# Attention's sums of values taken for two blocks of queries at a time, and the weights of values 192 bytes further in their tiles

## The chip, the core and the metric

One core of a Trainium2 chip runs the whole program in one launch. The metric is the time of one execution on the device in microseconds (us); 2318.97 is the median of three runs of the kernel before. TensorE (PE in the profile) multiplies matrices: it loads a stationary operand (PEld rows) and streams a moving operand past it into PSUM. VectorE (DVE), ScalarE (ACT) and GpSimd (POOL) do the elementwise work, and SyncE (SP) issues the transfers.

## The reference

Two token sequences of 1024 x 1024 (a "prompt" and a "sample") go through two layers with shared weights. The first layer is a mix of retention heads and a state-space branch; the change meets it only in the tiles of its weights. The second is a neighbourhood attention of 16 heads of 64 over a 16 x 64 grid of tokens:

```python
def _odd_mixer(h, w_in, w_out, rel_bias):
    q, k, v, g = jnp.split(h @ w_in, 4, axis=-1)
    o = _neighbourhood_attention(q.reshape(hs), k.reshape(hs), v.reshape(hs), rel_bias)
    return (o * jax.nn.silu(g)) @ w_out
...
        s = jnp.einsum('bqhd,brkhd->bhqrk', qr, kb).astype(jnp.float32) * scale
        s = s + jnp.transpose(bias, (0, 2, 1, 3))[None]
        s = jnp.where(col_valid[:, None, :], s, NEG_INF)
        p = jax.nn.softmax(s.reshape(B, H, GRID_W, kr * GRID_W), axis=-1)
        return jnp.einsum('bhqrk,brkhd->bqhd', p, vb)
```

Before each layer the input is normalized, scaled and shifted; after it the result is normalized, gated and added to the input.

## The kernel before

**Precision.** A product of an activation h and a weight w is made of three matmuls in the type fp32r: w's rounded part times h's rounded part, and each one's rounded part times the other's rest (`dense`, `values`). So every block of 512 KB of weights is loaded into a tile `wr`, copied by ScalarE into `wh` (rounded) and subtracted by VectorE or GpSimd into `wl` (the rest), in `split`. `wr` has two buffers, `wh` and `wl` three each, all of 4096 bytes a partition. `dense` has the weights as the stationary operand and 512 columns of h moving: 24 matmuls for one half (512 tokens) of one block of 128 output columns. `values` makes v with its tokens on the partitions, so there h is the stationary operand and 256 columns of `wh` or `wl` move.

**Attention's steps.** `layer1` projects q, k, v and the gate for eight pairs of heads in each of two sequences (s = 0, 1), and after every half of a block of `dense` (and every quarter of `values`) it calls `unit`, which takes one step of the generator `na_mix`. A step deals with three blocks of 128 queries of one pair of heads at once. There are 8 blocks in a pair and 16 pairs, so 128 blocks, and the step i takes in this order

- the sums of values of block i-2: the transposed probabilities `pt0` and `pt1` move past 64 columns of `vn` (one for each head of the pair, each into its own half of the partitions of the PSUM bank `psc`, so the array is used as 128 x 64). That is 4 matmuls where the block is the first or last of its pair (2 tiles of keys) and 6 elsewhere (3 tiles of keys); the profile shows twice as many, since a matmul in plain fp32 is run in two passes;
- after four blocks, the product of `psc` with the gate `g2` on VectorE (L1253) and its store into `oD`;
- the transposes of block i-1 (`na_turn`, L136 into `psb`, copied to `pt0` by ScalarE and to `pt1` by VectorE);
- the scores of block i (`na_scores`: `psa`, L1199 adds the bias and finds the least, ACT's L1201 takes the exponential, L1202 and L1203 normalize on VectorE).

Then the next 24 (or 48) matmuls of the projection follow, and then the next step.

**What sets the order.** In `layer1` every matmul is held in the order of the program (`pin`), so TensorE's order is that of the code. The other engines' order is found by the framework's scheduler, which simulates the program. Between the two sequences, `load_h` brings the second sequence's h in over the first's; its copies run on ScalarE, VectorE and GpSimd. At the end the steps that are left are woven into `out_proj` of the first sequence, 12 matmuls between steps. Here both spans have names: the **seam** (the change of sequences) and the **weave**.

**Memory.** `MAP_L1` says in which 4096-byte slots (A0 to A21) and 8192-byte slots (E0 to E3) of SBUF the attention's tiles stand: `pt0` and `pt1` have two buffers each, in E3. Pools are laid out one behind another, the pool `w` (`wr`, `wh`, `wl`) ahead of all slots.

Of the kernel before, what the change touches and what calls it, by code (L numbers as in the profile page):

```python
# [13 lines left out]
F32R = mybir.dt.float32r  # L14
# [5 lines left out]
P = 128  # L20
# [18 lines left out]
def _parts(text):  # L39
# [39 lines left out]

MAP_L1 = _parts(  # L80
# [3 lines left out]
MAP_L1.update(  # L84
    kh0=_fulls("A11 A13"), kh1=_fulls("A16 A17"), q0=_fulls("A8 A3"), q1=_fulls("A4 A5"),
# [32 lines left out]
class Trunk:  # L118
# [89 lines left out]
        e = self.nc.gpsimd if eng == "P" else self.nc.vector  # L208
        e.tensor_tensor(lo, raw, hi.bitcast(F32), SUB)  # L209

    def w_block(self, src, shape, eng):
        raw = self.ring(self.wpool, shape, "wr")
        hi = self.ring(self.wpool, shape, "wh", F32R, 3)
        lo = self.ring(self.wpool, shape, "wl", F32R, 3)
        self.load(raw, src)
        self.split(hi, lo, raw, eng)
        return hi, lo
# [43 lines left out]

    def queue_values(self, w, c0):
        self.todo += [partial(self.w_block, w[512 * j:512 * j + 512, c0:c0 + 2 * P].rearrange("(k p) c -> p k c", p=P),
                              [P, 4, 256], "P") for j in range(2)]

    def values(self, vn, scale, done=None):

# [760 lines left out]
    def out_weights(self, w, ph, blks):  # L1028
        for k in range(8):
            tag = f"ow{k}"  # L1030
            raw = self.t([P, 1024], "st", F32, ph) if "st" in ph.map and k > 3 else self.ring(self.wpool, [P, 1024], "wr")
            if tag not in ph.map:
                hi, lo = (self.ring(self.wpool, [P, 1024], x, F32R, 3) for x in ("wh", "wl"))
            elif len(ph.map[tag]) == 1:
                hl = self.t([P, 2, 1024], tag, F32R, ph)
                hi, lo = hl[:, 0], hl[:, 1]
            else:
                hi, lo = (self.t([P, 1024], tag, F32R, ph) for _ in range(2))
            self.load(raw, w[k * P:(k + 1) * P, :])
            self.split(hi, lo, raw, "V" if k in (1, 3, 5, 6) else "P")  # L1040
            blks.append((hi, lo))
            yield
# [180 lines left out]
    def na_mix(self):  # L1223

        sbs, pts = {}, {}
        raw = first = mid = last = po = None
        n = 8 * 16
        for i in range(-2, n + 2):
            k, j = divmod(i + 2, 8)
            if k < 16:  # L1230
                if j == 0:
                    if not k:
                        raw = self.na_raw(0)
                    first = self.na_bias(raw, "bl", self.mask[1], P, EDGE)
                elif j == 1:
                    mid = self.na_bias(raw, "bm", self.mask[0], 0, WIDE)
                elif j == 2:
                    last = self.na_bias(raw, "br", self.mask[1], 0, EDGE)
                elif j == 3 and k < 15:
                    raw = self.na_raw((k + 1) % 8)  # L1240
            if 0 <= i - 2 < n:
                k, j = divmod(i - 2, 8)
                if j % 4 == 0:
                    po = self.pst("c")
                pt, b0 = pts.pop(i - 2), max(j - 1, 0)
                nk = 3 if 0 < j < 7 else 2
                for z in range(nk):
                    for a in range(2):
                        self.mm(po[64 * a:64 * a + 64, (j % 4) * P:(j % 4 + 1) * P], self.na[k]["vn"][:, b0 + z, 64 * a:64 * a + 64],
                                pt[a][:, z * P:(z + 1) * P], start=(z == 0), stop=(z == nk - 1))  # L1250
                if j % 4 == 3:
                    o, sl = self.t([P, 512], "o"), slice((j - 3) * P, (j + 1) * P)
                    self.nc.vector.tensor_tensor(o, po, self.na[k]["g2"][:, sl], MUL)  # L1253
                    s, p = divmod(k, 8)
                    self.store(self.oD[1, s][p * P:(p + 1) * P, sl], o)
            if 0 <= i - 1 < n:
                pts[i - 1] = self.na_turn(sbs.pop(i - 1), (i - 1) % 8)
            if 0 <= i < n:
                k, j = divmod(i, 8)
                sbs[i] = self.na_scores(self.na[k], first if j == 0 else last if j == 7 else mid, j)  # L1260
            yield
# [239 lines left out]
```

## Time and profile before

| what | value |
|---|---|
| median of 3 runs (lowest to highest) | 2318.97 us (2318.91 to 2320.42) |
| the profiled execution's own time | 2319.64 us |
| its span, first to last instruction | 2317.8 us |
| mean granted clock of TensorE | 0.984 |
| busy: PE, PEld, DVE, ACT, POOL | 96%, 80%, 59%, 37%, 34% |
| chain that ended last, by engine | PE 72%, DVE 11%, DMA 8%, POOL 3% |

The profiled execution is 0.67 us above the median. Layer 0 takes the first half of the span; attention's steps run from about 1187 us to about 2163 us of it, and the last `out_proj` ends the program. A busy PE is only a sign that something is in its pipeline: matmuls overlap, so what one costs is read from the starts of neighbours, not from its duration.

### The profile page before, as it was taken

The numbers are of one execution on the slowest core, as the hardware profiler recorded it, in microseconds if no ns is written. First come the engines' busy times: TensorE is split into PE (matmuls) and PEld (weight loads), VectorE is DVE, ScalarE is ACT, GpSimd is POOL, SyncE is SP. The second block draws the span as 40 slices with busy tenths as digits, with TensorE's granted clock in tenths as the row PEclk, the third lists the DMA queues.
The fourth block names the chain that finished last, engine by engine and source line by source line (L and its number), as shares of the span: only waits on it lengthen the run. The fifth ranks groups of instructions, "written<-read, shape, count | busy, mean of one in ns | idle before, by whom it ended". The sixth has DMA issues, their size and how long they took to land.

```text
span 2317.8 us, 35213 instructions
## 1 busy us (share of the span) xinstructions
PE 2216.5 (96%) x13248; PEld 1844.3 (80%) x13248; DVE 1374.4 (59%) x3013; ACT 853.7 (37%) x1842; POOL 785.1 (34%) x670
## 2 busy tenths in 40 slices
PE   6989988998999999999999999998999999998997
PEld 4757877786878888888988888887888888886786
DVE  4836888888899566575345545455545545457322
ACT  4532321223322244343344434355444444444211
POOL 2335555657665121456511111113111101113233
PEclk9999999999999999999999999999999999999999
DMA  9774232224221245435511111224111111114354
GB/s 316 248 229 135 74 88 45 67 81 139 56 64 52 85 157 184 164 132 177 150 39 53 53 52 45 62 56 82 57 42 53 53 53 53 40 55 150 88 141 121
DMA packets 296481, 231.14 MB, mean 100 GB/s; under 512 B 58488, under 2 KB 267768, under 8 KB 296312
## 3 DMA queue, kind: packets, MB, share of 16 engines
q1 hardware_dynamic: 296312, 228.90, 33.1%
q8 instruction: 105, 1.72, 0.3%
q14 instruction: 64, 0.52, 0.1%
HBM read 169.92 MB, written 56.84 MB: 98 GB/s over the span
## 4 chain that ended last, share of the span: by engine, by line
PE 72%; DVE 11%; DMA 8%; POOL 3%; issue 2%; SPq 2%; ACT 2%; DVEq 0%; POOLq 0%; ACTq 0%
PE psd L131 52%; PE psc L131 5%; DMA out_y<-h_lo 5%; PE psa L131 4%; PE psb L136 4%; DVE E L767 2%; PE psz L131 2%; SPq L191 2%; PE psy L131 2%; PE psb L131 1%; POOL E L764 1%; DMA oD<-A 1%; PE pse L131 1%; DVE E L1203 1%; DMA wn<-in_w_mod 1%
## 5 line engine op out<-in xcount | busy, mean ns | idle before, releaser
L131 PE MATMUL psd<-h_hi,wh 128*128 128x512 f32 x1392 | 555.5, 400 | 0.7 <-DVE h_hi L454 0.5
L131 PE MATMUL psd<-h_lo,wh 128*128 128x512 f32 x1392 | 547.9, 394 | 0.4 <-DVE h_lo L456 0.4
L131 PE MATMUL psd<-h_hi,wl 128*128 128x512 f32 x1392 | 546.4, 393 | 0.0
L131 PEld LDWEIGHTS psd<-h_hi,wh 128*128 128x128 f32 x1392 | 264.0, 190 | 57.1 <-issue 3.7
L131 PEld LDWEIGHTS psd<-h_hi,wl 128*128 128x128 f32 x1392 | 263.3, 189 | 57.1 <-issue 1.2
L131 PEld LDWEIGHTS psd<-h_lo,wh 128*128 128x128 f32 x1392 | 263.7, 189 | 55.4 <-issue 2.9
L131 PE MATMUL psd<-wh,h_hi 128*128 128x256 f32 (+1 forms) x960 | 284.1, 309 | 0.0
L131 PE MATMUL psd<-wl,h_hi 128*128 128x256 f32 (+1 forms) x864 | 255.9, 296 | 0.0
L198 ACT ACTIVATE wh<-wr 128x1024 fp32r<-128x1024 f32 x118 | 124.5, 1056 | 342.1 <-PE psd L131 251.1
L209 POOL TENSOR_TENSOR wl<-wr,wh 128x1024 fp32r<-128x1024 f32 x51 | 125.5, 2461 | 293.3 <-ACT wh L198 293.0
L131 PE MATMUL psd<-wh,h_lo 128*128 128x256 f32 x768 | 217.5, 283 | 0.0
L131 PEld LDWEIGHTS psd<-wh,h_hi 128*128 128x128 f32 x960 | 184.5, 192 | 8.2 <-issue 0.2
L1201 ACT ACTIVATE E<-E,nm 128x368 f32<-128x368 f32 (+1 forms) x256 | 146.4, 573 | 91.0 <-DVE nm L1199 90.1
L131 PEld LDWEIGHTS psd<-wl,h_hi 128*128 128x128 f32 x864 | 166.2, 192 | 4.1 <-POOL wl L209 0.5
L1219 DVE COPY E<-psb 128x384 f32<-128x384 f32 (+1 forms) x128 | 66.5, 520 | 140.8 <-PE psb L136 139.3
L1181 POOL TENSOR_TENSOR A<-A,A 128x256 f32<-128x256 f32 (+1 forms) x80 | 56.2, 725 | 274.7 <-DVE nm L1199 270.4
L131 PEld LDWEIGHTS psd<-wh,h_lo 128*128 128x128 f32 x768 | 147.6, 192 | 0.3
L209 DVE TENSOR_TENSOR wl<-wr,wh 128x1024 fp32r<-128x1024 f32 x67 | 90.6, 1352 | 84.7 <-ACT wh L198 84.4
L1203 DVE TENSOR_SCALAR E<-E,su 128x368 f32<-128x368 f32 (+1 forms) x256 | 131.2, 513 | 9.0
L136 PE MATMUL psb<-ident,E 128*128 128x128 f32 x704 | 107.8, 286 | 19.8 <-DVE E L1203 16.8
L1199 DVE CUSTOM_DVE_ANT_0 E<-psa,A 128x368 f32<-128x368 f32 (+1 forms) x256 | 121.7, 504 | 4.7 <-PE psa L131 3.7
L389 DVE TENSOR_TENSOR rs<-ss 128x1 f32<-128x1 f32 x64 | 38.9, 608 | 120.6 <-ACT h_lo L1099 57.7
(336 smaller groups left out, 4183.7 us busy)
## 6 DMA issues: line engine op xcount, KB each, us to landing
wr<-in_w_in_c SPq DMA_DIRECT2D x64, 512.0 KB
wr<-in_w_in_ab SPq DMA_DIRECT2D x48, 512.0 KB
wr<-oD SPq DMA_DIRECT2D x32, 512.0 KB
wn<-in_w_mod SPq DMA_DIRECT2D x24, 512.0 KB
wm<-in_w_mod SPq DMA_DIRECT2D x8, 1024.0 KB
hD<-A SPq DMA_DIRECT2D x32, 256.0 KB
ox<-in_x SPq DMA_DIRECT2D x16, 512.0 KB
x1D<-ox SPq DMA_DIRECT2D x16, 512.0 KB
```

What stands on the lines that cost most here:

```text
L131: i = self.nc.tensor.matmul(*a, **k)
L136: i = self.nc.tensor.transpose(*a, **k)
L191: i = self.nc.sync.dma_start(dst, src)
L198: self.nc.scalar.activation(dst, src, AF.Copy, scale=scale)
L209: e.tensor_tensor(lo, raw, hi.bitcast(F32), SUB)
L389: self.nc.vector.tensor_tensor(rs, ss[:, 0:1], ss[:, 1:2], ADD)
L767: Vv.tensor_tensor_scan(t1[:, q], r8, t1[:, q], 0.0, MUL, ADD)
L1181: self.nc.gpsimd.tensor_tensor(b, raw[a][:, c0:c0 + n], mask, ADD)
L1199: Vv.tensor_tensor_reduce(sn, sc[a], bt[a], -1.0, 3.0e38, ADD, ALU.min, nm)
L1201: nc.scalar.activation(sn, sn, AF.Exp, bias=nm, scale=-1.0, accum_out=su)
L1203: Vv.tensor_scalar(sn, sn, su, None, MUL)
L1219: self.nc.vector.tensor_copy(pt, pp)
```

## The change

`na_mix` now takes the sums of values only in its odd steps, for the blocks i-3 and i-2 one behind the other; even steps have none. `pt0` and `pt1` get four buffers each: two in E3 as before, and one each in the slots A19 and A20, which layer 1 did not use. The tiles `wh` and `wl` become 1088 elements (4352 bytes) wide instead of 1024 (4096 bytes), and the split weights of values stand 48 elements, 192 bytes, behind a tile's start; all other weights stand at its start. So the six tiles of `wh` and `wl` follow each other at 4352 bytes instead of 4096, and all that lies behind them moves up by 1536 bytes.

```diff
-    "E3 pt0 1536 pt0 1536 pt1 1536 pt1 1536 o 2048; A7 bm0 1472 bm1 1472 bl0 1024;"
+    "E3 pt0 1536 pt0 1536 pt1 1536 pt1 1536 o 2048; A19 pt0 1536 pt1 1536; A20 pt0 1536 pt1 1536; A7 bm0 1472 bm1 1472 bl0 1024;"
...
+    def w_tile(self, tag, shape, off=0):
+
+        w = self.ring(self.wpool, [P, 1088], tag, F32R, 3)[:, off:off + 1024]
+        return w.rearrange("p (a b) -> p a b", a=shape[1]) if len(shape) > 2 else w
+
+    def w_block(self, src, shape, eng, off=0):
         raw = self.ring(self.wpool, shape, "wr")
-        hi = self.ring(self.wpool, shape, "wh", F32R, 3)
-        lo = self.ring(self.wpool, shape, "wl", F32R, 3)
+        hi, lo = (self.w_tile(x, shape, off) for x in ("wh", "wl"))
...
-                              [P, 4, 256], "P") for j in range(2)]
+                              [P, 4, 256], "P", 48) for j in range(2)]
...
-            if 0 <= i - 2 < n:
-                k, j = divmod(i - 2, 8)
-                if j % 4 == 0:
-                    po = self.pst("c")
-                pt, b0 = pts.pop(i - 2), max(j - 1, 0)
-                nk = 3 if 0 < j < 7 else 2
-                for z in range(nk):
-                    for a in range(2):
-                        self.mm(po[...], self.na[k]["vn"][...], pt[a][...], ...)
+            if i >= 3 and i % 2:
+                for b in (i - 3, i - 2):
+                    k, j = divmod(b, 8)
+                    if j % 4 == 0:
+                        po = self.pst("c")
+                    pt, b0 = pts.pop(b), max(j - 1, 0)
+                    nk = 3 if 0 < j < 7 else 2
+                    for z in range(nk):
+                        for a in range(2):
+                            self.mm(po[...], self.na[k]["vn"][...], pt[a][...], ...)
```

The operands of the matmul are cut in this diff; they are the same on both sides. Up to the first of these steps, every engine's instructions stand in the same order as before.

On TensorE, the first place where the order differs is step 2 (block 0's sums of values) and step 3 (block 1's). Before, a row of sums stands between the projection (`psd`) and the transposes (`psb`) in each:

```order
L131 MATMUL psd_10163<-h_hi,wl_9969 128x512
L131 MATMUL psc_10196<-E_1067_10043,vn_1025_9607 64x128 x4
L136 MATMUL psb_10201<-ident,E_1023_9598 128x128 x3
...
L131 MATMUL psd_10229<-h_hi,wl_9969 128x512
L131 MATMUL psc_10196<-E_1067_10043,vn_1025_9607 64x128 x6
L136 MATMUL psb_10272<-ident,E_1023_9598 128x128 x3
```

Now, at the same places:

```order
L131 MATMUL psd_10163<-h_hi,wl_9969 128x512
L136 MATMUL psb_10196<-ident,E_1023_9598 128x128 x3
...
L131 MATMUL psd_10224<-h_hi,wl_9969 128x512
L131 MATMUL psc_10261<-E_1067_10043,vn_1025_9607 64x128 x10
L136 MATMUL psb_10272<-ident,E_1023_9598 128x128 x3
```

Block 0's four matmuls moved behind block 1's projection, where ten stand together; the transposes of step 2 now follow the projection at once.

On VectorE, the place is step 13, in which the sums of the blocks 8 to 11 are multiplied with the gate (`TENSOR_TENSOR ...<-psc`), ahead of the copy of transposed probabilities and of the next scores (`ISA` is L1199's custom instruction). Before:

```order
L1203 TENSOR_SCALAR E_1023_9598<-E_1023_9598,su_10986 128x368
L1253 TENSOR_TENSOR E_1023_9598<-psc_10821,g_1115_10325 128x512
L209 TENSOR_TENSOR wl_11017<-wr_11015,wh_11016 128x1024
L1219 COPY E_1067_10043<-psb_11040 128x384
L1199 ISA E_1023_9598,nm_11051<-psa_11045,A_1062_10009 128x368
```

Now:

```order
L1207 TENSOR_SCALAR E_1023_9598<-E_1023_9598,su_10982 128x368
L209 TENSOR_TENSOR wl_11013<-wr_11011,wh_11012 128x1024
L1259 TENSOR_TENSOR E_1023_9598<-psc_10886,g_1116_10326 128x512
L1147 SCALAR_TENSOR_TENSOR E_1022_9596<-psd_10986,kh_1208_10950 64x512
L1223 COPY E_1067_10043<-psb_11042 128x384
```

The split of a weight block (`wl`) now stands ahead of the product with the gate, and one step of k's evacuation (`kh`) ahead of the copy.

## Rows read from the trace of the kernel before

**Rows 1.** Page, part 5: the costliest group; busy us, mean ns.

```profile
L131 PE MATMUL psd<-h_hi,wh 128*128 128x512 f32 x1392 | 555.5, 400 | 0.7 <-DVE h_hi L454 0.5
```

**Rows 2.** Windows of attention: length, then each engine's busy us, clock, DMA.

```profile
1186.50:1556.00 369.50, 369.50 (x2437) 314.85 (x2436) 185.77 (x518) 163.54 (x375) 54.94 (x48) 1.00 0.17 51
1556.00:1607.00 51.00, 42.77 (x256) 35.74 (x254) 34.23 (x63) 34.10 (x50) 17.01 (x7) 0.93 0.53 104
1607.00:2086.00 479.00, 479.00 (x3136) 407.24 (x3135) 242.68 (x675) 212.31 (x487) 70.41 (x63) 1.00 0.16 50
2086.00:2164.00 78.00, 66.38 (x404) 52.34 (x403) 50.22 (x118) 33.11 (x80) 21.88 (x13) 0.91 0.42 125
```

**Rows 3.** Timeline, PE, step 1, which has no sums: start us, us.

```profile
1186.62 0.39 PE L131 MATMUL psd<-h_hi,wl 128*128 128x512 f32 x1
1186.85 0.60 PE L136 MATMUL psb<-ident,E 128*128 128x128 f32 x4
1187.20 0.41 PE L131 MATMUL psa<-kh,q 128*128 128x368 f32 x1
...
1187.94 0.39 PE L131 MATMUL psd<-h_hi,wh 128*128 128x512 f32 x1
...
1188.65 0.39 PE L131 MATMUL psd<-h_hi,wh 128*128 128x512 f32 x1
...
1193.20 0.39 PE L131 MATMUL psd<-h_hi,wl 128*128 128x512 f32 x1
```

**Rows 4.** Timeline, PE, a later step: eight passes of sums behind a projection of values.

```profile
1247.85 0.28 PE L131 MATMUL psd<-wl,h_hi 128*128 128x256 f32 x1
1248.06 0.66 PE L131 MATMUL psc<-E,vn 128*64 128x128 f32 x8
1248.65 0.66 PE L136 MATMUL psb<-ident,E 128*128 128x128 f32 x4
1249.06 0.41 PE L131 MATMUL psa<-kh,q 128*128 128x368 f32 x1
```

**Rows 5.** Timeline, PE, a step with twelve passes of sums behind a dense projection.

```profile
1262.58 0.39 PE L131 MATMUL psd<-h_hi,wl 128*128 128x512 f32 x1
1262.89 0.88 PE L131 MATMUL psc<-E,vn 128*64 128x128 f32 x12
1263.70 0.88 PE L136 MATMUL psb<-ident,E 128*128 128x128 f32 x6
1264.33 0.41 PE L131 MATMUL psa<-kh,q 128*128 128x368 f32 x1
```

**Rows 6.** Waits of PE in the weave (total, times, longest); timeline of the weave and seam.

```profile
PE psb L136 <- DVE E L1203: 11.6, 6, 3.3
...
2122.34 0.87 PE L136 MATMUL psb<-ident,E 128*128 128x128 f32 x3 [3.14 <-DVE E L1203]
...
1603.71 1.51 PE L136 MATMUL psb<-ident,E 128*128 128x128 f32 x6 [3.06 <-DVE su L1202]
```

**Rows 7.** Timeline, step 14: the last normalization, and the transposes that need it.

```profile
1285.00 0.41 DVE L1203 TENSOR_SCALAR E<-E,su 128x368 f32<-128x368 f32 x1
...
1286.98 0.77 PE L136 MATMUL psb<-ident,E 128*128 128x128 f32 x5
```

**Rows 8.** Groups by line and form: one of the three matmuls of values.

```profile
L131 PE MATMUL psd<-wh,h_lo 128*128 128x256 f32 x768 | 217.5, 283 | 0.0
```

**Rows 9.** One run of 48 matmuls of values: load durations (ns), first and third start.

```profile
L131 PEld LDWEIGHTS psd<-wh,h_lo x16: 188/192/192, 1242.2 to 1247.6; 128*128 128x128 f32 x16
...
1242.22 0.28 PE L131 MATMUL psd<-wh,h_hi 128*128 128x256 f32 x1
...
1242.45 0.28 PE L131 MATMUL psd<-wl,h_hi 128*128 128x256 f32 x1
```

**Rows 10.** Timeline, PE, layer 0: the last of a run of values, and what follows.

```profile
232.62 0.28 PE L131 MATMUL psd<-wl,h_hi 128*128 128x256 f32 x1
232.74 0.28 PE L131 MATMUL pse<-sel,A 128*128 128x2 f32 x2
```

More of the change, by code (lines that the diff above doesn't have):

```diff
@@ L209, in split @@
         e.tensor_tensor(lo, raw, hi.bitcast(F32), SUB)
-    def w_block(self, src, shape, eng):
+    def w_tile(self, tag, shape, off=0):
+        w = self.ring(self.wpool, [P, 1088], tag, F32R, 3)[:, off:off + 1024]
+        return w.rearrange("p (a b) -> p a b", a=shape[1]) if len(shape) > 2 else w
+    def w_block(self, src, shape, eng, off=0):
         raw = self.ring(self.wpool, shape, "wr")
-        hi = self.ring(self.wpool, shape, "wh", F32R, 3)
-        lo = self.ring(self.wpool, shape, "wl", F32R, 3)
+        hi, lo = (self.w_tile(x, shape, off) for x in ("wh", "wl"))
         self.load(raw, src)
@@ L1032, in out_weights @@
             if tag not in ph.map:
-                hi, lo = (self.ring(self.wpool, [P, 1024], x, F32R, 3) for x in ("wh", "wl"))
+                hi, lo = (self.w_tile(x, [P, 1024]) for x in ("wh", "wl"))
             elif len(ph.map[tag]) == 1:
@@ L1240, in na_mix @@
                     raw = self.na_raw((k + 1) % 8)
-            if 0 <= i - 2 < n:
-                k, j = divmod(i - 2, 8)
-                if j % 4 == 0:
-                    po = self.pst("c")
-                pt, b0 = pts.pop(i - 2), max(j - 1, 0)
-                nk = 3 if 0 < j < 7 else 2
-                for z in range(nk):
-                    for a in range(2):
-                        self.mm(po[64 * a:64 * a + 64, (j % 4) * P:(j % 4 + 1) * P], self.na[k]["vn"][:, b0 + z, 64 * a:64 * a + 64],
-                                pt[a][:, z * P:(z + 1) * P], start=(z == 0), stop=(z == nk - 1))
+            if i >= 3 and i % 2:
[7 more added lines that the diff above has]
+                        for a in range(2):
+                            self.mm(po[64 * a:64 * a + 64, (j % 4) * P:(j % 4 + 1) * P],
+                                    self.na[k]["vn"][:, b0 + z, 64 * a:64 * a + 64],
+                                    pt[a][:, z * P:(z + 1) * P], start=(z == 0), stop=(z == nk - 1))
                 if j % 4 == 3:
```

## The prediction

> **What bounds the kernel now.** I read the costliest groups first, then a table of windows over the attention, then the timeline of single steps, and at last the waits. The costliest groups are the matmuls of the projections: one of the three kinds of `dense` alone is busy for 555.5 us [rows 1]. The windows say where that is a bound. From 1186.5 to 1556 us and from 1607 to 2086 us PE is busy for the whole of the window, at a granted clock of 1.00, while DVE is busy for about half of it and ACT for 44% [rows 2]. In these 848 us whatever TensorE need not do comes off the end. In the seam (1556 to 1607) PE is busy for 42.77 of 51 us, in the weave (2086 to 2164) for 66.38 of 78, and the clock falls to 0.93 and 0.91: there something else ends last. The waits name it: transposes that wait for VectorE's normalization, six times in the weave, 11.6 us together [rows 6]. A microsecond of TensorE's work that goes from such a step is not saved, since it stood inside the wait.
>
> **The visits to the sums of values.** The timeline shows what one visit costs, as the way from the last matmul of the projection to the first score. Without a visit, with four transposes, it is 1187.20 - 1186.62 = 0.58 us [rows 3]. With eight passes of sums it is 1249.06 - 1247.85 = 1.21 us; the matmul ahead is one of values, whose next neighbour starts 0.12 later rather than 0.23 as in rows 3, so 1.32 on the same footing [rows 4]. The visit costs 0.74. A pass costs (0.88 - 0.66) / 4 = 0.055, by the groups of twelve and of eight [rows 4, 5]; eight are 0.44, so 0.30 belongs to the visit as such. The step with twelve passes agrees: 1.75 us, against 0.58 and another 0.22 for six transposes instead of four, is 0.95, less 12 x 0.055 = 0.66 leaves 0.29 [rows 3 to 5]. I take 0.30. It lies on the way in (0.31 us from the last matmul to the first pass, where 0.23 is usual), in the first passes and on the way out.
>
> The change keeps all passes and halves the visits: 128 blocks have 128 visits now, one in each of the steps 2 to 129, and 64 afterwards. Of the 64 that go (the even steps), 24 lie in the first full window and 31 in the second (counted by the groups of transposes between the bounds), 3 in the seam and 6 in the weave. The 55 in the full windows save 55 x 0.30 = 16.5 us. In the weave the waits of rows 6 belong to the transposes of the blocks 117, 119, 121 and 125, and all four of these are even steps. There the visit goes from inside a wait, which gets longer by as much, and its passes come back in the next step in the open: 12 x 0.055 = 0.66 us lost each, 2.6 us. The other two pairs of the weave (blocks 123 and 127) have no wait and save 0.30 each. In the seam a chain of copies for the second sequence's h bounds the whole; of its three pairs I count one as lost (the wait of 3.06 us at 1603.71 is block 53's, an even step again [rows 6]) and the others at nothing. Sum: 16.5 + 0.6 - 2.6 - 0.7 = 13.8 us saved.
>
> **What is late next in the even steps.** Their transposes now follow the projection at once, 0.74 to 0.95 us sooner after the scores that feed them. The tightest block that I found in the full windows is 13 of its sixteen: its normalization ends at 1285.00 + 0.41 = 1285.41, the transposes begin at 1286.98, and those of the second head, the fourth of six, some 0.4 us later [rows 7]. That leaves 1.9 us, and 1.0 after the change. It is also the step in which VectorE's order changes (the split of a weight block goes ahead of the product with the gate). The same instructions stand ahead of the scores in both orders, so I cost this at nothing; what it costs if that cover goes is the second rival. The four buffers of `pt0` and `pt1` take no wait away and add none: a buffer is written again four blocks later, at least a whole step after its last reader. The sums of a step's second block read tiles that were copied a projection earlier, as before. The store of four blocks comes in the same step as before, behind six more passes.
>
> **The 192 bytes.** Nothing is added; three times 768 = 2304 matmuls of values read their moving operand from another place [rows 8]. The trace of before has no such place for these tiles, so I bound it. In a run of 48, the third starts at 1242.45 and the last at 1247.85: 5.40 / 45 = 0.120 us each. The first two steps take 0.23, 0.115 each, and the loads of the stationary operand last from 188 to 192 ns within this run [rows 4, 9]. So 0.005 us each are there to be had at least at times: 2304 x 0.005 = 11.5 us is the one end. The other is the dearest beginning among the neighbours, three dense steps in 0.71 us (0.237) against 20 in 4.55 (0.2275) [rows 3]: 0.009 more, 21 us lost. I take zero, by the nearest row. In layer 0 the last matmul of such a run stands ahead of a small one whose stationary tile `modr` begins 1120 + 1120 + 1152 = 3392 bytes into its slot, which is off the multiples of 512 at which the tiles of h, `wh` and `wl` stand, and at the very distance of 192 from them, modulo 512, that the change makes. Its neighbour starts 0.12 later, as in the rest of the run [rows 10].
>
> The Trainium skill has a rule against this half of the change: "SBUF — State Buffer", section "Who interferes with whom", gives TensorE a read port for the moving operand and another, independent one for weight loads, and says that it waits on nobody. By that rule the place is worth nothing and the sum stays as it is; the loads of 188 to 192 ns in one run [rows 9] show that something varies which the rule does not name, though not that it is the place. The Trainium skill's "TensorE: Matmul & The Clock Gate", section "Back-to-back issue gap", has N / 2.4 + 2.5 ns, which would be 109 ns for 256 columns; an estimate by that page, if the new place reached it, is 2304 x 0.011 = 25 us.
>
> **Sum.** The profiled execution took 2319.64 us, 0.67 above the median of 2318.97. 2319.64 - 13.8 = 2305.8, and on the footing of the median 2305. Its own range is 2301 to 2312: the fixed cost of a visit within 0.02 either way (1 us), the seam and the weave within 4.
>
> **Rivals.**
>
> First, the place counts as well: the loads of values no longer meet the moving reads, and their 2304 matmuls keep the pace of a run's first steps. For it speaks that pace itself [rows 9]; against it rows 10. It saves 11.5 us more: 2294; with all of the spread, where a step is rounded to 0.01, down to 2284.
>
> Second, the full windows start to wait. In the even steps the normalization comes later than the 1.0 us that is left allows, because VectorE's order puts a split (`wl`) ahead of the product with the gate. Each of the eight steps of the kind of rows 7 would lose what exceeds 1.0 us. If the split and the product, some 1.9 us together, are both in the way, that is 0.9 us in 8 steps and less in 8 more, some 9 us: 2314, and with longer waits in the weave 2316, which is no change. Against it: VectorE is idle for half of the window [rows 2].
>
> Third, slower: the new pitch of 4352 bytes sets the second tile of `wh` and the first and third of `wl` off the multiples of 512 (256 past them), and `dense`, with `wh` in two of three matmuls, then reads 2/3 x 1/3 + 1/3 x 2/3 = 4/9 of its 3 x 1392 = 4176 weights there. If these 1856 and the 2304 of values all keep the dear beginning's pace, 0.009 us more [rows 3], it costs 37 us against the 13.8: 2342. It decides from 13.8 / 4160 = 0.0033 us a matmul. For it speaks only that the pace varies at all.
>
> **How the numbers follow.** My forecast 54%, the first rival 28%, the second 10%, the third 8%. A measurement of this kernel can tell about 0.2%, 4.6 us, from no change. Forecast and first rival are faster (82%), the second is within 0.2% (10%), the third slower (8%). The range takes in the first two cases and the better part of the second rival: 2285 to 2315.
>
> **What would show it.** In the profile after: 64 groups of sums instead of 128, of 16 to 24 passes, each starting 0.31 us after the last matmul of the projection; in even steps transposes 0.23 us behind the projection. The windows of attention with PE still wholly busy, 7 and 9 us shorter. In the weave the waits at the same four blocks, each longer by up to 0.9. The matmuls of values 0.12 us apart: 0.115 would be the first rival, and with it some 3 us more in layer 0's share of them. Waits for L1207 (L1203 before) in the full windows would be the second; dense steps above 0.23 in every second block the third. I am wrong if the full windows shorten by less than 12 us, or if the pace of values moves.

## The result, and the profile after

The changed kernel takes 2291.24 us (median of four runs, 2285.23 to 2293.26) against 2319.66 (four runs, 2318.91 to 2320.42): a ratio of 0.9875, with a 95% interval of 0.986 to 0.989. That is 28.4 us less, where 13.8 were forecast. The time lies in the range, but it is the first rival's (2294), not the forecast's (2305, with a range of its own from 2301 to 2312): the range held only because it took that rival in. The profiled execution is the fastest of the four, 2285.23 us, 6 us under the median.

First the windows, cut at the first transpose of the blocks 0, 48, 54, 115 and 127 (length, then each engine's busy us with its instructions, clock, DMA share, GB/s):

```profile
1178.18:1536.27 358.09, 358.09 (x2426) 312.90 (x2424) 185.46 (x515) 161.94 (x374) 54.86 (x48) 1.00 0.18 52
1536.27:1592.86 56.59, 48.82 (x320) 42.93 (x318) 35.75 (x69) 36.04 (x56) 18.67 (x8) 0.94 0.48 94
1592.86:2046.66 453.80, 453.80 (x3036) 395.29 (x3035) 238.69 (x659) 207.17 (x475) 68.97 (x61) 1.00 0.17 52
2046.66:2125.28 78.62, 66.60 (x410) 55.09 (x409) 51.06 (x126) 33.00 (x80) 21.88 (x13) 0.91 0.44 129
```

As in [rows 2], PE is busy for the whole of the two full windows, the first and the third row: no new wait came in. The same cuts in the trace of before, and in those of three experiments described below, give this table (us; the last column ends at the start of the last group of matmuls):

| kernel | block 0 starts at | 0 to 48 | 48 to 54 (seam) | 54 to 115 | 115 to 127 (weave) | 127 to last |
|---|---|---|---|---|---|---|
| before | 1186.85 | 367.70 | 58.50 | 466.52 | 79.82 | 145.31 |
| after | 1178.18 | 358.09 | 56.59 | 453.80 | 78.62 | 145.89 |
| pairs of blocks alone | 1190.29 | 360.40 | 56.77 | 456.50 | 78.96 | 145.89 |
| 192 bytes alone | 1185.09 | 365.29 | 59.32 | 463.71 | 78.78 | 145.31 |
| four blocks at a time | 1180.59 | 354.58 | 56.38 | 449.62 | 70.79 | 147.19 |

The full windows give 9.6 + 12.7 = 22.3 us. Block 0 starts 8.7 us sooner, but that column moves from execution to execution: in kernels whose layer 0 differs in nothing but the place of values or of h it lies between 1178 and 1193. Only what the place explains (below) is counted there.

Now an odd step and the even one behind it, on PE in the timeline (start us, us, instruction), for [rows 3 to 5]:

```profile
1260.94 0.39 PE L131 MATMUL psd<-h_hi,wh 128*128 128x512 f32 x1
...
1266.17 0.39 PE L131 MATMUL psd<-h_hi,wl 128*128 128x512 f32 x1
1266.49 1.53 PE L131 MATMUL psc<-A,vn 128*64 128x128 f32 x24
1267.95 0.87 PE L136 MATMUL psb<-ident,E 128*128 128x128 f32 x6
1268.58 0.41 PE L131 MATMUL psa<-kh,q 128*128 128x368 f32 x1
...
1274.59 0.39 PE L131 MATMUL psd<-h_hi,wl 128*128 128x512 f32 x1
1274.82 0.82 PE L136 MATMUL psb<-ident,E 128*128 128x128 f32 x6
1275.39 0.41 PE L131 MATMUL psa<-kh,q 128*128 128x368 f32 x1
```

Twenty-four passes stand in one visit. From the last matmul of the projection to the first score the odd step needs 1268.58 - 1266.17 = 2.41 us; the prediction's numbers make it 0.58 + 0.22 + 0.30 + 24 x 0.055 = 2.42. The even step, with no visit, needs 0.80, and 0.58 + 0.22 was the estimate. The first two rows hold the 24 matmuls of one half of `dense`: (1266.17 - 1260.94) / 23 = 0.2274 us each, what it was before (0.2275).

Values did change their pace. Two runs of 48 of them in the timeline, first and last matmul of each, for the run of [rows 9]:

```profile
1209.47 0.28 PE L131 MATMUL psd<-wh,h_hi 128*128 128x256 f32 x1
...
1215.00 0.28 PE L131 MATMUL psd<-wl,h_hi 128*128 128x256 f32 x1
...
1216.45 0.28 PE L131 MATMUL psd<-wh,h_hi 128*128 128x256 f32 x1
...
1221.78 0.28 PE L131 MATMUL psd<-wl,h_hi 128*128 128x256 f32 x1
```

The first run keeps 5.53 / 47 = 0.1177 us a matmul, the second 5.33 / 47 = 0.1134; in [rows 4, 9] it was 0.120. In the calls of layer 1 outside the seam the first and the fourth run of the four keep the one pace and the second and the third the other, 0.1157 on the mean; the kernel with the 192 bytes alone (below) has the same order of paces. The group of [rows 8] says the same, 214.4 us for 217.5:

```profile
L131 PE MATMUL psd<-wh,h_lo 128*128 128x256 f32 x768 | 214.4, 279 | 0.0
```

Last the waits, for [rows 6]: PE's waits in the weave in all, and the four of them in the timeline (blocks 117, 119, 121 and 125; in brackets the idle time and its releaser):

```profile
PE psb L136 <- DVE E L1207: 12.0, 4, 3.7
```

```profile
2062.60 0.85 PE L136 MATMUL psb<-ident,E 128*128 128x128 f32 x6 [3.29 <-DVE E L1207]
...
2074.54 1.33 PE L136 MATMUL psb<-ident,E 128*128 128x128 f32 x4 [2.19 <-DVE E L1207]
...
2088.11 1.51 PE L136 MATMUL psb<-ident,E 128*128 128x128 f32 x6 [2.77 <-DVE E L1207]
...
2112.94 1.51 PE L136 MATMUL psb<-ident,E 128*128 128x128 f32 x6 [3.74 <-DVE E L1207]
```

The same four blocks wait, as forecast, but together for 12.0 us instead of 11.6, not for 3.8 more.

### The profile page after: what moved, and what is told of

Its sections match the earlier page's. It is cut to its first block, busy times and chain, and to the rows that moved or that the text cites. A ratio compares the mean times of both kernels' runs of the same rounds, so it can differ in the third digit from the quotient of the medians.

```text
span 2283.5 us, 35173 instructions
## 1 busy us (share of the span) xinstructions
PE 2183.2 (96%) x13248; PEld 1838.0 (80%) x13248; DVE 1371.3 (60%) x3013; ACT 850.4 (37%) x1842; POOL 786.0 (34%) x670
## 4 chain that ended last, share of the span: by engine, by line
PE 73%; DVE 11%; DMA 8%; POOL 2%; issue 2%; SPq 2%; ACT 2%; DVEq 0%; POOLq 0%; ACTq 0%
PE psd L131 53%; DMA out_y<-h_lo 5%; PE psc L131 4%; PE psa L131 4%; PE psb L136 4%; PE psz L131 2%; SPq L191 2%; DVE E L771 2%; PE psy L131 2%; PE psb L131 2%; DMA oD<-A 1%; POOL E L768 1%; PE pse L131 1%; DVE A L666 1%; ACT h_hi L198 1%
## 5 line engine op out<-in xcount | busy, mean ns | idle before, releaser
L131 PE MATMUL psd<-wh,h_lo 128*128 128x256 f32 x768 | 214.4, 279 | 0.0
L209 DVE TENSOR_TENSOR wl<-wr,wh 128x1024 fp32r<-128x1024 f32 x67 | 90.5, 1351 | 118.2 <-ACT wh L198 117.9
L1207 DVE TENSOR_SCALAR E<-E,su 128x368 f32<-128x368 f32 (+1 forms) x256 | 127.8, 501 | 8.7
L136 PEld LDWEIGHTS psb<-ident,E 128*128 128x128 f32 x704 | 80.4, 143 | 39.3 <-issue 25.0
```

The costliest lines, as they stand in the source:

```text
L131: i = self.nc.tensor.matmul(*a, **k)
L136: i = self.nc.tensor.transpose(*a, **k)
L1207: Vv.tensor_scalar(sn, sn, su, None, MUL)
```

## The experiments

**Pairs of blocks alone.** The changed kernel with tiles of 4096 bytes and the values at their start:

```diff
-        w = self.ring(self.wpool, [P, 1088], tag, F32R, 3)[:, off:off + 1024]
+        w = self.ring(self.wpool, [P, 1024], tag, F32R, 3)
...
-                              [P, 4, 256], "P", 48) for j in range(2)]
+                              [P, 4, 256], "P", 0) for j in range(2)]
```

> The sums of values in pairs as in the change, but the weights' tiles at their old pitch of 4096 bytes and the weights of values at the tile's start. Theory (visits and place each pay on their own): 64 visits fewer at 0.29 us, with the weave no dearer, 16.5 to 18.5 us off the median of before, 2301 to 2303; values stay 0.120 us apart. Rival (the pairs pay for nearly all of the 28 us, the place only shows in the spacing): below 2295.

Measured: 2301.21 us (2297.72 to 2302.18) against 2321.93 of the kernel before on the same chip, a ratio of 0.9906 (0.9889 to 0.9922), 20.7 us. That is 2.2 us more than the 16.5 to 18.5 expected; the traces account for 19.3 (below). Values keep 0.120. Its two full windows, cut as above:

```profile
1190.29:1550.69 360.40, 360.40 (x2425) 315.20 (x2424) 185.39 (x515) 161.92 (x374) 54.70 (x48) 1.00 0.18 52
...
1607.40:2064.00 456.60, 456.60 (x3039) 398.00 (x3036) 238.60 (x659) 207.17 (x475) 68.78 (x61) 1.00 0.17 51
```

The first full window is 7.3 us shorter than before: 24 visits x 0.30 = 7.2. The second is 10.0 shorter than 466.52 (by the table): 31 x 0.30 = 9.3, and one block's 12 passes (0.66) that stand before the cut in the old order and behind it in the new. Both terms hold.

**192 bytes alone.** The kernel before with the wider tiles and the values 192 bytes into them, the sums one block at a time:

```diff
-        hi = self.ring(self.wpool, shape, "wh", F32R, 3)
-        lo = self.ring(self.wpool, shape, "wl", F32R, 3)
+        hi, lo = (self.w_tile(x, shape, off) for x in ("wh", "wl"))
...
-                              [P, 4, 256], "P") for j in range(2)]
+                              [P, 4, 256], "P", 48) for j in range(2)]
```

> The 192 bytes and the new pitch alone; the sums of values one block a step, as before. Theory: values 0.1155 us apart instead of 0.1198, 2304 x 0.0043 = 10 us off: 2309 to 2311. Rival (place pays nothing in time): 2318 to 2320. Rival (the pitch alone gains in dense as well): dense steps under 0.2275 and the time under 2307.

Measured: 2310.52 us (2305.39 to 2315.54), a ratio of 0.9951 (0.9931 to 0.997), 11.4 us. The full windows are 2.4 and 2.8 us shorter than before, and they hold 12 and 14 runs of 48 values: 2.4 / 576 and 2.8 / 672 are both 0.0042 us a matmul, and 2304 of them make 9.6. `dense` keeps 0.228. So the place is worth about what the first rival said, and the dearer `dense` of the third is not seen.

**Is it the place or the distance?** The changed kernel with 192 bytes of unused memory ahead of h and the values at the start of their tiles, which are 4096 bytes wide again, so that both operands move and the distance between them is what it was:

```diff
+            nc.vector.memset(act.tile([P, 48], F32, name="shift"), 0.0)
```

> Pairs as in e1, and 192 bytes of unused memory ahead of h, so that h and the weights both stand 192 bytes off the grid and their distance is 0 as in the kernel before. Theory A (distance counts): values 0.120 us apart. Theory B (the moving operand's own place counts): 0.1155.

Measured: 2312.12 us in one run, whose layer 0 is late (block 0 at 1192.94); values take 0.1199 each. The group, first of this kernel, then of the one with 192 bytes alone:

```profile
L131 PE MATMUL psd<-wh,h_lo 128*128 128x256 f32 x768 | 217.8, 284 | 0.0
```

```profile
L131 PE MATMUL psd<-wh,h_lo 128*128 128x256 f32 x768 | 215.4, 281 | 0.0
```

The gain is gone when both move. What counts is how far the moving weights stand from the stationary h, modulo some number of bytes, not where they stand.

**Which distances.** Each of the twelve calls of `values` with another one:

```diff
+SWEEP = [2, 4, 60, 64, 0, 8, 16, 24, 32, 40, 48, 56]
...
+        off = SWEEP[self.vcall]
+        self.vcall += 1
...
-                              [P, 4, 256], "P", 48) for j in range(2)]
+                              [P, 4, 256], "P", off) for j in range(2)]
```

> The change with another place for the weights of each of the twelve projections of values: 8, 16, 240 and 256 bytes behind the tile's start for the four of layer 0, then 0, 32, 64, 96, 128, 160, 192 and 224 bytes for the eight of layer 1. Theory A (what counts is the distance of the moving weights from the stationary h, modulo 256 bytes or less): 0 and 256 give 0.120 us, 192 gives 0.1155, and the others lie between or below in a smooth order with a best place. Theory B (any place off the 512-byte grid will do): all but 0 and 256 give 0.1155. Theory C (the line of 16 bytes counts): 8 differs from 16, and 16 equals 192.

and once more with `[12, 14, 20, 36, 42, 44, 46, 47, 49, 50, 52, 54]`:

> As the first sweep, at 48, 56, 80 and 144 bytes (layer 0), and 168, 176, 184, 188, 196, 200, 208 and 216 (layer 1). Theory A: a smooth order around the best place; if a run of values settles into one of two paces at 192 (0.1135 or 0.1178 us, by how it began), a neighbour of 192 should settle into the faster one alone, or a little above. Rival: 192 is best and its neighbours fall off on both sides.

Measured, one run each (2295.54 and 2293.5 us), mean ns from one matmul of values to the next (steps above 150 ns left out):

| bytes | 0 | 8 | 16 | 32 | 48 | 56 | 64 | 80 | 96 | 128 | 144 | 160 |
|---|---|---|---|---|---|---|---|---|---|---|---|---|
| ns | 119.9 | 120.0 | 118.7 | 116.7 | 118.4 | 120.0 | 116.7 | 120.0 | 119.9 | 118.6 | 118.2 | 117.7 |

| bytes | 168 | 176 | 184 | 188 | 192 | 196 | 200 | 208 | 216 | 224 | 240 | 256 |
|---|---|---|---|---|---|---|---|---|---|---|---|---|
| ns | 119.9 | 119.2 | 120.0 | 115.6 | 115.7 | 120.1 | 119.9 | 118.4 | 121.2 | 118.3 | 117.2 | 119.9 |

Two runs of 48 in the second sweep's timeline, at 184 and at 188 bytes (first and last matmul of each), and under them the loads of the stationary operand in the run at 184 (ns: least, median, most):

```profile
1333.97 0.28 PE L134 MATMUL psd<-wh,h_hi 128*128 128x256 f32 x1
...
1339.60 0.28 PE L134 MATMUL psd<-wl,h_hi 128*128 128x256 f32 x1
...
1454.15 0.28 PE L134 MATMUL psd<-wh,h_hi 128*128 128x256 f32 x1
...
1459.58 0.28 PE L134 MATMUL psd<-wl,h_hi 128*128 128x256 f32 x1
```

```profile
L134 PEld LDWEIGHTS psd<-wh,h_hi x16: 187/188/188, 1333.8 to 1339.2; 128*128 128x128 f32 x16
```

5.63 / 47 = 0.1198 against 5.43 / 47 = 0.1155: four bytes decide. A mean can hide several paces, though. At 8 bytes the four runs of 48 keep 120.0, 116.9, 116.9 and 126.0 ns, at 64 bytes one keeps 113.3 and three 117.8 or 117.9. So a distance does not fix one pace, and what chooses among them was not tried. Of the theories only the period of 256 bytes stands (0 and 256 are alike, and so are the tiles of one call, which lie 256 bytes apart); no order in the distances is to be seen inside it. And the loads last 188 ns in the slow run: their duration, in which the prediction saw a sign of the pace, does not tell it.

**The same for dense.** The weights of `dense` at 0 to 224 bytes, in steps of 32 from call to call:

```diff
+        self.dcall += 1
+        off = 8 * (self.dcall % 8)
```

> The change, with the weights of the dense projections at 0, 32, 64, 96, 128, 160, 192 and 224 bytes behind their tiles' start in turn (values stay at 192). Theory (distance counts only where the load of the stationary operand is as long as the matmul): dense steps stay at 0.2267 us at all eight. Rival (distance counts wherever loads meet moving reads): dense steps differ by place, by some 0.004 us.

Measured, one run (2297.76 us), mean ns from one matmul of `dense` to the next (steps above 280 ns left out), by the place of the weights: 227.9 at 0, 229.4 at 192, 232.5 at 128, 233.1 at 224 and 233.3 to 233.9 at 32, 64, 96 and 160. Here the weights are the stationary operand, so weights 192 bytes further mean that the moving h stands 192 behind them, which is 64 modulo 256. Two halves in the timeline, with the weights at 224 and at 0 bytes:

```profile
1245.98 0.40 PE L132 MATMUL psd<-h_hi,wh 128*128 128x512 f32 x1
...
1251.35 0.39 PE L132 MATMUL psd<-h_hi,wl 128*128 128x512 f32 x1
...
1261.21 0.39 PE L132 MATMUL psd<-h_hi,wh 128*128 128x512 f32 x1
...
1266.47 0.39 PE L132 MATMUL psd<-h_hi,wl 128*128 128x512 f32 x1
```

5.37 / 23 = 0.2335 against 5.26 / 23 = 0.2287. Here the expected answer was wrong: `dense` depends on the distance too, and at its own, 0, it is best of the eight. The third rival's mechanism therefore exists; the new pitch escaped it because it shifts tiles by 256 bytes, which counts as 0.

**Fewer visits still.** The changed kernel with the sums of four blocks in every fourth step:

```diff
-            if i >= 3 and i % 2:
-                for b in (i - 3, i - 2):
+            if i >= 5 and i % 4 == 1:
+                for b in range(i - 5, i - 1):
```

> The change with the sums of four blocks in every fourth step: 32 visits instead of 64, the same passes and buffers. Theory (a visit costs 0.29 us wherever TensorE is the bound, and nothing else): 28 of the 32 further visits lie in the full windows or save there, 8 us less than the change, 0.984 of before, with up to 2 us more lost or won in the weave. Rival (the saving is used up, since three steps of four now have no sums in front of their transposes and four blocks stand in one): no faster than the change, 0.9875.

Measured: 2271.13 us (2270.04 to 2273.47) against 2316.24, a ratio of 0.981 (0.9786 to 0.9833): faster than both kernels. By the table the full windows lose another 3.5 and 4.2 us, 7.7 for some 27 visits, again 0.29 each. More than expected came from the weave: 7.8 us to block 127, 6.5 to the last matmul. Its waits there:

```profile
PE psb L136 <- DVE E L1207: 5.1, 3, 3.1
PE psb L136 <- DVE su L1206: 2.5, 2, 1.9
```

That is 7.6 us for 12.0. The waits at the blocks 121 and 125 alone, 2.77 and 3.74 us in the changed kernel, are 4.0 us shorter:

```profile
2081.00 1.10 PE L136 MATMUL psb<-ident,E 128*128 128x128 f32 x6 [0.63 <-DVE su L1206]
...
2102.37 1.40 PE L136 MATMUL psb<-ident,E 128*128 128x128 f32 x6 [1.88 <-DVE su L1206]
```

In the changed kernel one normalization (L1207) of each of these blocks takes 2.52 us beside an addition on GpSimd (last section); here they take 0.41 and 1.23. The mean granted clock of the weave, block 115 to 127, is 0.95 here and 0.91 there.

**Where does that come from?** Four blocks at a time up to block 115, pairs in the weave:

```diff
+            if i >= 5 and i % 4 == 1 if i < 118 else i % 2:
+                for b in (range(i - 5, i - 1) if i < 118 else (i - 3, i - 2)):
```

> Sums of four blocks in every fourth step up to block 115, pairs of blocks from there on (the weave). The kernel with four blocks throughout was 7.7 us shorter than the changed kernel in the two full windows and 8.9 us in the weave. If the fixed cost of a visit makes the 7.7 us and the weave's 8.9 us come from the steps woven there (fewer of them stand in a wait), this kernel keeps the 7.7 and loses the 8.9: some 2280 us, with waits of about 12 us in the weave. Rival: the 8.9 us come from how far VectorE's earlier work has got by then; then this kernel keeps most of them: 2271 to 2274, with waits of 5 to 8 us.

Measured: 2284.42 us (2282.26 to 2288.17), a ratio of 0.9842 (0.9827 to 0.9857). The windows keep the gain (354.58 and 449.59), the weave loses it (78.35 to block 127), and its waits are 10.1 us, less than the 12 expected of it but with 2.77 and 3.75 at the blocks 121 and 125 again, each behind a normalization of 2.52 us. The clock of the weave is 0.91 again. (The 8.9 us of the expectation run from block 116 to 127.) So the gain in the weave belongs to the steps there, not to a head start of VectorE. The traces show three things in it: the two normalizations, the waits behind them, and the clock; how the microseconds split among them was not tried.

**The pairs in the weave.** The changed kernel, from block 116 on one block at a time:

```diff
-            if i >= 3 and i % 2:
-                for b in (i - 3, i - 2):
+            if i >= 3 and (i % 2 or 118 <= i < n + 2):
+                for b in ((i - 3, i - 2) if i < 118 else (i - 2,)):
```

> The changed kernel, except that from step 118 on (blocks 116 to 127, the weave) every step takes the sums of one block, as the kernel before did. My prediction counted the pairs in the weave as a net loss of 2 us (2.6 lost in four waits, 0.6 saved). If that term holds, the way from the transposes of block 115 to the last matmul is some 2 us shorter here than the 136.2 us of the changed kernel (2271.17 less 2134.97 or so), and the normalization waits of the weave fall below its 12.0 us. Rival: the pairs lose nothing there, because the waits' length is set by VectorE and GpSimd and not by TensorE; then this stretch is the same within 0.5 us or up to 1.5 us longer (in the kernel before it was 1.2 us longer), and the time is 2291 to 2294.

Measured: 2294.8 us (2288.12 to 2296.78), a ratio of 0.9888 (0.9871 to 0.9904), so the whole program shows no difference from the change. The stretch of the expectation, whose length is misstated there, runs from 2046.66 to 2271.17 us in the changed kernel, 224.51, and takes 222.47 here: 2.04 less, which is the prediction's 2.0 to the digit. It comes from something else. The table of windows around block 125's wait, first after, then this kernel:

```profile
2109.00:2122.00 13.00, 9.26 (x54) 7.74 (x53) 6.92 (x15) 2.52 (x10) 2.34 (x1) 0.74 0.32 85
```

```profile
2114.00:2125.00 11.00, 7.70 (x60) 6.19 (x59) 7.69 (x17) 2.93 (x9) 2.34 (x1) 1.00 0.32 89
```

and the steps behind that wait in the two timelines, after first:

```profile
2115.47 0.63 PE L131 MATMUL psd<-wh,h_hi 128*128 128x512 f32 x1
2115.90 0.63 PE L131 MATMUL psd<-wl,h_hi 128*128 128x512 f32 x1
...
2119.87 1.53 PE L131 MATMUL psc<-E,vn 128*64 128x128 f32 x24
```

```profile
2118.82 0.52 PE L136 MATMUL psb<-ident,E 128*128 128x128 f32 x3 [3.30 <-DVE E L1207]
...
2119.86 0.39 PE L131 MATMUL psd<-wh,h_hi 128*128 128x512 f32 x1
2120.09 0.40 PE L131 MATMUL psd<-wl,h_hi 128*128 128x512 f32 x1
...
2122.68 0.88 PE L131 MATMUL psc<-E,vn 128*64 128x128 f32 x12
```

In the changed kernel the clock stands at the lower of its levels (1.2 GHz) behind the wait of 3.74 us, and matmuls of 512 columns start 0.43 us apart; here it stays at the upper (2.4 GHz), 0.23 apart, behind one of 3.30. From the end of the wait to the next sums it is 2119.87 - 2112.94 = 6.93 us there and 2122.68 - 2118.82 = 3.86 here, of which 0.5 are transposes done ahead of the wait: some 2.5 us are the clock's, more than the whole difference. In the kernel before, 3.31 us at the same block, the longest wait of [rows 6], were followed by the lower level too (a mean of 0.76):

```profile
2147.41 0.87 PE L136 MATMUL psb<-ident,E 128*128 128x128 f32 x3 [3.31 <-DVE E L1203]
```

```profile
2143.00:2157.00 14.00, 10.69 (x62) 8.70 (x59) 8.28 (x19) 3.15 (x11) 2.34 (x1) 0.76 0.30 81
```

With the 192 bytes alone, where TensorE has the order of the kernel before, the same wait is 3.30 us and the upper level follows (1.00 from 2138 to 2152 us). So the length of these waits does not decide it. Six executions that share the order of the changed kernel take 224.05 to 226.17 us for this stretch. A term of 2 us can't be read from it.

## Why the prediction came out as it did

**Right: the visits.** 55 x 0.30 = 16.5 was the forecast; pairs alone gave 7.3 + 10.0 - 0.66 = 16.6. It held because [rows 2] show TensorE without a gap there, and because the even steps' 1.0 us of slack was enough: no wait for L1207 in either window. The second rival falls, and VectorE's new order (split ahead of the product) did no harm.

**Wrong: "I take zero, by the nearest row", for the 192 bytes.** It measured 9.6 us, and the pace moved, which the prediction had named as a sign of being wrong. The nearest row was one neighbour at the distance of 192, 0.12 us behind its predecessor [rows 10]. One gap rounded to 0.01 cannot tell 0.1157 from 0.120; and the sweeps show that nearness in bytes says little, since 188 and 184 differ by 4.4 of the 5.6 ns that lie between the extremes of the table. The better reading stood beside it: 0.115 in a run's first steps [rows 9] and the end of 11.5 us made from it, which held. The first rival was right that the place counts. Its reason, loads that no longer meet the moving reads, is not shown: what was shown is a dependence on the distance between the operands.

The rule that spoke for zero, in the Trainium skill's "SBUF — State Buffer", section "Who interferes with whom" (two independent read ports, TensorE waits on nobody), does not cover this: the runs give 0.0042 us a matmul by distance alone, and the measurement decides. The estimate of 25 us, by the formula of the Trainium skill's "TensorE: Matmul & The Clock Gate", section "Back-to-back issue gap" (there for an isolated matmul), was not reached either.

**Wrong: the weave's loss of 2.0 and the seam's of 0.7.** Pairs alone saved 1.7 us in the seam (within what other executions of that order move, 56.6 to 58.5), and the weave with what follows lost nothing that can be read: 225.13 us before, 224.85 with pairs. The step that failed is "the wait gets longer by as much". It nearly did so at block 117 (two waits of 1.43 and 1.13 us before, 3.29 after), but at 119 the wait hardly moved (2.33 to 2.19; 2.65 with pairs alone), at 121 it fell by 0.4 (3.14 to 2.77) and at 125 it grew by 0.4 only (3.31 to 3.74). At block 121 VectorE's timeline shows a reason, first in the kernel with single blocks in the weave, then after:

```profile
2085.69 0.69 DVE L1259 TENSOR_TENSOR E<-psc,g 128x512 f32<-128x512 f32 x1 [2.30 <-PE psc L131]
2086.30 1.22 DVE L209 TENSOR_TENSOR h_hi<-wr,h_hi 128x1024 fp32r<-128x1024 f32 x1
2087.43 0.42 DVE L1223 COPY E<-psb 128x256 f32<-128x256 f32 x1
```

```profile
2080.81 1.23 DVE L209 TENSOR_TENSOR h_hi<-wr,h_hi 128x1024 fp32r<-128x1024 f32 x1 [2.21 <-ACT h_hi L198]
...
2082.02 0.68 DVE L1259 TENSOR_TENSOR E<-psc,g 128x512 f32<-128x512 f32 x1
2082.62 0.41 DVE L1223 COPY E<-psb 128x256 f32<-128x256 f32 x1
```

With single blocks VectorE stands idle for the sums, then multiplies, then splits, and only then comes the copy ahead of the scores' chain. With pairs the sums come later, so the scheduler put the split ahead of the product, into that idle time. From the block's first score to its last transpose it takes 8.31 us with singles (2085.98 to 2094.29) and 7.52 with pairs (2081.68 to 2089.20). Of these 0.8 us the earlier copy makes some 0.5 (it starts 0.94 us behind the first score with pairs, 1.45 with singles); VectorE's order differs in other places too, and the rest is not split. The prediction costed this same exchange at nothing; in a stretch that waits for VectorE it was worth some 0.5 us.

**The sum.** 16.6 for the full windows, 1.7 for the seam and 0.9 for the weave with its carried passes make 19.3 us (before rounding) in the trace of pairs alone, 20.7 by the medians; with 9.6 for the distance (11.4 by the medians) that is 28.9, and 28.4 were measured.

## What to carry to other kernels

Where the timeline shows TensorE without a gap, a visit to matmuls of another shape (here 128 x 64 between 128 x 128) can be priced from the starts of neighbours, 0.29 to 0.30 us whether two or four blocks share it, and removed by batching. That the change of the array's shape is what costs in a visit was not tried apart. The distance between the stationary and the moving operand of a matmul is a parameter to sweep, form by form and in small steps, many values in one kernel; the best of one form is a bad one for the other (0 bytes: 227.9 ns, the best for `dense`, and 119.9 for values, where the best is 115.6). Where TensorE waits, compare the clock behind the waits before giving a difference of a few microseconds to the change.

## What was not expected of the hardware

- The pace of a matmul depends on the byte distance of its operands, 0 and 256 being alike: 115.6 to 121.2 ns on the mean of four runs of 48 with 256 columns moving (113.3 to 126.0 in single runs), 227.9 to 233.9 with 512. At 192 bytes two paces occur, 113.4 and 117.7 ns, fixed within a run; at 8 bytes three. What makes the order of the distances, and what chooses a pace, stays open.
- A normalization on VectorE that usually takes 0.41 us took 2.52 beside an addition on GpSimd; it stands in front of block 121's wait, and another of 2.52 in front of block 125's, in the kernel before and in the changed one too. From the kernel with single blocks in the weave, VectorE and GpSimd in the timeline:

```profile
2089.34 0.41 DVE L1207 TENSOR_SCALAR E<-E,su 128x368 f32<-128x368 f32 x1
...
2091.17 2.52 DVE L1207 TENSOR_SCALAR E<-E,su 128x368 f32<-128x368 f32 x1
```

```profile
2091.15 2.34 POOL L1117 TENSOR_TENSOR h_lo<-h_lo 128x1024 f32<-128x1024 f32 x1 [1.62 <-DVE su L1206]
```

  GpSimd starts 0.02 us ahead and ends at 2093.49, VectorE at 2093.69. The Trainium skill's "SBUF — State Buffer", section "Who interferes with whom", lets one of the two block the other for a whole instruction through a shared pair of ports, and the rows agree: VectorE is done 0.20 us behind GpSimd. With four blocks throughout, the additions no longer start together with a normalization, and the two waits fell to 0.63 and 1.88 us; moving the addition by itself was not tried.
- Waits of much the same length (3.30 and 3.31 us) at the same block were followed by the upper level of the clock in one execution and by the lower in another, also where TensorE's order is the same (3.30 with the 192 bytes alone, 3.31 before).
